# A mixture-of-experts stage with a written matmul order, smaller gather batches, more load buffers and another last norm

## The chip, the cores and the metric

The kernel runs on one core of one Trainium2 chip, as one program. The time is device microseconds of that core; lower is better. A time given is the median of repeated runs; the profile is one further execution with its own time. Engines are named as in the profile: PE is TensorE (PEld its weight loads), DVE VectorE, ACT ScalarE, POOL GpSimd, SP SyncE.

## The reference, cut to what matters

256 tokens of 1024 numbers pass through two dense blocks (feed-forward, state-space and attention mixers, feed-forward) and then a third block, whose end is what the change touches:

```python
h = h + ga1 * y                        # y: the mixer's output, merged @ w_out
u2 = rmsnorm(h, g_norm2) * (1 + sc2) + sh2
lg = u2 @ w_rg + b_rg                  # 4 groups
le = u2 @ w_re + b_re                  # 32 experts; top 2 inside the best group
comb = ...                             # (256, 32), two weights a token
for e in range(32):                    # D = 1024, d_expert = 512
    hid = silu(u2 @ w1[e]) * (u2 @ w3[e])
    y2 = y2 + comb[:, e:e+1] * (hid @ w2[e])
h = h + ga2 * y2
out = rmsnorm(h, g_final) * (1 + scf) + shf
```

All data are float32. Each of the 32 experts has three matrices of 2 MB, 192 MB in all.

## The kernel before

The dense blocks run from 0 to about 1517 us and are the same in both kernels but for the small reciprocal root (`rsqrt`, L71), which every norm calls. The products there are split into a high and a low part in a faster float32 format (three matmuls in place of one). What follows is the experts' stage.

**Loads.** `expert_loads` brings the 192 MB as 192 DMAs of 1 MB on SP's queue, in the order in which they are used: for each pair of experts w1 (4 loads), w3 (4), and w2 of the pair before (4). They go into a ring of buffers: 3 in `stream2`, 2 in `stream3`, 4 in `stream`, 3 in the stage's own pool (RAW2, RAW3, RAWB, RAW4), 12 in all. A load is issued when PE has read out what its buffer held before; `halves` asks for two new ones whenever two are used up.

**Before the first expert.** The last product of the mixer, with `w_out`, is made in two halves of 512 columns (L958 to L985). After each half DVE makes the new residual `x` and the gained rows `xg`, PE turns `xg` and multiplies it with the router's matrix (L980). Then `prep_end` makes `rstd`, DVE the router's logits `lg` (L989), `norm2` the normed rows: two DVE operations over 1024 columns (L1335), high parts on ACT (L1340), low parts on POOL (L1341). `route` picks two experts a token in some twenty small DVE operations (L1205 to L1241), and counts with two matmuls which of the 64 slots of an expert each token takes (`pos`). `gather` then makes a 0/1 matrix `sel` and with it, by matmul (L1431), the rows of 8 experts at a time, 64 slots each (CAP = 64, BATCH = 8), into a tile T.

**A pair of experts.** `project` multiplies w1 and then w3 with the gathered rows (L1469): one expert's 64 slots stand in the lower half of PE's columns and the other's in the upper half, so that matmuls of the two run side by side if they are issued one after the other. `hidden` turns the results (L1484) and makes silu times up; `down` multiplies with w2 of the pair before (L1504); ACT and DVE scale the result into a high and a low part (`yh` L1512, `yl` L1513); `spread` adds it to four PSUM tiles `acc` by eight matmuls with the turned 0/1 matrix (L1522). `slots` (L1446, L1448) makes that matrix and the slots' weights. PE's order in all this is chosen by a list scheduler at build time, which moves single matmuls into what it takes to be gaps; `beside` and `tick` offer it the gather and spread work.

**The end.** `finish` multiplies the four `acc` tiles by the gate `ga2` (L1365), jumps over the code for experts with more than 64 tokens (`overflow`, not entered with these inputs), adds to `x` (L1370, DVE), squares on ACT (L1371), multiplies by the gain on POOL (L1372), takes the root with `rsqrt` (12 small DVE operations), and makes the output in four pieces (L1377), stored by four DMAs (L1380). `finish_rows` loads and combines the rows for this on POOL while `route` runs.

Of the kernel before, what the change touches and what calls it, by code (L numbers as in the profile page):

```python
# [19 lines left out]
P = 128  # L20
D = 1024
# [5 lines left out]
NEXP = 32  # L27
CAP = 64
RAWB = 4
HLB = 3  # L30
RAW2 = 3
RAW3 = 2
RAW4 = 3
BATCH = 8
# [14 lines left out]
class Kern:  # L49
# [21 lines left out]
    def rsqrt(self, src, n, scale, pool=None):  # L71

        nc, pool = self.nc, pool or self.small
# [7 lines left out]
            y.bitcast(I32), t.bitcast(I32), -1.0, float(0x5F3759DF), op0=ALU.mult, op1=ALU.add  # L81
        )
        for _ in range(3):
            nc.vector.tensor_mul(t, y, y)  # L84
            nc.vector.scalar_tensor_tensor(t, t, -0.5, m, op0=ALU.mult, op1=ALU.mult)  # L85
            nc.vector.scalar_tensor_tensor(y, t, 1.5, y, op0=ALU.add, op1=ALU.mult)  # L86
# [742 lines left out]
    def mixer2(self):  # L829
        nc, a, tc = self.nc, self.a, self.tc  # L830
        w_in = a["w_in_2"][0]
        with ExitStack() as outer:
# [124 lines left out]
            self.ss = self.t(self.small, [P, 2, 2], "ss", bufs=2)  # L957
            pl = [self.t(self.ax, [P, 512], "ax") for _ in range(2)]  # L958
            xTs = self.t(keep, [P, 2, D], "o")
            for nb in range(2):  # L960
                sl = slice(nb * 512, (nb + 1) * 512)
                ps = self.gemm_x(a["w_out_2"][0], nb * 512, 512, self.xh, self.xl)
                xT = xTs[:, nb, :].rearrange("p (c t) -> p c t", c=4)
                done = None
                for t in range(2):
                    with tc.issue_after(done) if done else ExitStack():
                        m = self.t(self.tmp, [P, 512], "xg")
                        nc.vector.tensor_mul(m, ps[t], ga1[:, sl])
# [228 lines left out]
    def route(self, pool):  # L1197
# [36 lines left out]
        nc.vector.tensor_add(mb, o1, o2)  # L1234
# [3 lines left out]
        nc.tensor.matmul(pp[:, 32:64], self.ones, mb[:, 0, :], start=False, stop=True)  # L1238
        pos = self.t(pool, [P, 2, 32], "pos")
# [36 lines left out]
    def moe_begin(self):  # L1276
# [5 lines left out]
        w = self.t(self.s2, [P, 4, D], "T")  # L1282
        self.xg, self.sh2 = w[:, 0:2, :], w[:, 2, :]
        nc.gpsimd.dma_start(self.sh2, self.modd[0:1, 3 * D : 4 * D].to_broadcast([P, D]))
# [25 lines left out]
    def moe_final(self):  # L1310
        nc, a, tc = self.nc, self.a, self.tc
        with ExitStack() as ctx:
# [9 lines left out]
            route = self.route(lp)  # L1322
            self.norm2(lp, u2h, u2l)
            pos = next(route)
            rows = self.finish_rows(lp)
            comb, cnt = self.experts(lp, u2h, u2l, route, pos, acc)
            self.finish(lp, acc, rows, cnt, comb)

    def norm2(self, lp, u2h, u2l):

        nc = self.nc
        w = self.t(lp, [P, 4, D], "T")
        for t in range(2):
            u = w[:, t, :]
            nc.vector.scalar_tensor_tensor(  # L1335
                u.rearrange("p (k q) -> p q k", k=KD), self.xg[:, t, :].rearrange("p (q k) -> p q k", k=KD),
                self.rstd[:, t : t + 1], self.sh2.rearrange("p (q k) -> p q k", k=KD),
                op0=ALU.mult, op1=ALU.add,
            )
# [3 lines left out]
    def finish_rows(self, lp):  # L1343
# [14 lines left out]
    def finish(self, pool, acc, rows, cnt, comb):  # L1358
# [5 lines left out]
        for t, nb, sl in parts:  # L1364
            nc.vector.tensor_mul(y[:, t, sl], acc[t][nb], ga2[:, sl])  # L1365
# [437 lines left out]
```

## Time and profile before

| what | value |
|---|---|
| median of 3 runs | 2054.01 us (2053.54 to 2054.9) |
| the profiled execution's own time | 2053.34 us |
| its span, first to last instruction | 2051.6 us |
| PE busy | 1967.1 us (96%) |
| DVE, ACT, POOL busy | 1226.8, 882.6, 138.5 us |
| moved by DMA | 493.11 MB, mean 240 GB/s |

In the profile's page a line of 40 digits gives each engine's busy share in slices of 51 us; the experts' stage is the last ten slices. PE's digit is 9 in nearly all of the span, and since a matmul's record covers its whole way through the array, a 9 does not say that no time is lost between matmuls. In the last ten slices the DMA digit is 9 as well, with some 420 GB/s. Line numbers in rows of before are those of the kernel before.

### The profile page before, as it was taken

Reading aid. Unit: us, or ns where it says so; the run is one execution under the profiler, and the core shown is the slowest. Engines: PE = TensorE matmul, PEld = TensorE weight load, DVE = VectorE, ACT = ScalarE, POOL = GpSimd, SP = SyncE. Lnnn points to the kernel's source line nnn. Section 1 sums busy time; section 2 is a strip of 40 time slices with the busy share of each in tenths; the row PEclk is TensorE's granted clock in tenths of the full one; section 3 lists DMA queues with packets and bytes.
Section 4 is the critical chain, followed back from the end, with each engine's and each line's share of the span. In section 5 each row is a group of like instructions: output and inputs, shape, how many; then the busy total and the mean of one; then the engine's idle time right before and its main releaser. Section 6 shows DMA issues by size and latency. Waiting matters only on the chain. (4 is left out here: it accounts for less than half of the span.)

```text
span 2051.6 us, 25322 instructions
## 1 busy us (share of the span) xinstructions
PE 1967.1 (96%) x9734; PEld 1436.8 (70%) x9734; DVE 1226.8 (60%) x2099; ACT 882.6 (43%) x1318; POOL 138.5 (7%) x226
## 2 busy tenths in 40 slices
PE   8999999999999999999999999999969999999996
PEld 6888978788888888887788888978754333333332
DVE  5884897778867775698866555999772111110113
ACT  5444676654444444575745444576522101111101
POOL 1000222000000000014000000000120000000001
PEclk9999999999999999999999999999989999999998
DMA  8885543447776885642446556544766999999994
GB/s 281 280 283 185 166 144 103 154 155 266 263 258 207 266 271 182 196 150 97 133 144 204 179 164 204 177 148 140 244 261 269 422 414 378 421 369 420 421 421 172
DMA packets 193100, 493.11 MB, mean 240 GB/s; under 512 B 11832, under 2 KB 47600, under 8 KB 168400
## 3 DMA queue, kind: packets, MB, share of 16 engines
q1 hardware_dynamic: 185760, 479.32, 64.6%
q0 software_dynamic: 4992, 11.49, 1.7%
q8 instruction: 78, 1.28, 0.2%
q10 hardware_dynamic: 2224, 0.66, 0.2%
q14 instruction: 46, 0.38, 0.1%
HBM read 490.34 MB, written 1.08 MB: 240 GB/s over the span
## 5 line engine op out<-in xcount | busy, mean ns | idle before, releaser
L128 DVE TENSOR_TENSOR lo<-raw,hi 128x1024 fp32r<-128x1024 f32 (+1 forms) x462 | 563.6, 1221 | 280.4 <-ACT hi L127 279.4
L127 ACT ACTIVATE hi<-raw 128x1024 fp32r<-128x1024 f32 (+1 forms) x462 | 486.6, 1055 | 548.4 <-PE mm L174 477.9
L172 PE MATMUL mm<-hi,xh 128*128 128x512 f32 (+2 forms) x1200 | 463.9, 388 | 3.7 <-ACT hi L127 3.7
L173 PE MATMUL mm<-lo,xh 128*128 128x512 f32 (+2 forms) x1200 | 458.3, 382 | 0.4 <-DVE lo L128 0.4
L174 PE MATMUL mm<-hi,xl 128*128 128x512 f32 (+2 forms) x1200 | 457.8, 381 | 0.0
L172 PEld LDWEIGHTS mm<-hi,xh 128*128 128x128 f32 x1200 | 226.0, 189 | 49.2 <-ACT hi L127 4.6
L173 PEld LDWEIGHTS mm<-lo,xh 128*128 128x128 f32 x1200 | 226.2, 188 | 46.3 <-DVE lo L128 2.0
L174 PEld LDWEIGHTS mm<-hi,xl 128*128 128x128 f32 x1200 | 226.0, 188 | 46.0
L1469 PE MATMUL mm<-raw,T 128*64 128x512 f32 x1024 | 242.4, 596 | 0.0
L1469 PEld LDWEIGHTS mm<-raw,T 128*64 128x64 f32 x1024 | 72.9, 137 | 139.8 <-issue 137.0
L1504 PE MATMUL mm<-raw,H 128*64 128x512 f32 x512 | 148.6, 600 | 10.1 <-DVE gu L1474 10.1
L172 PE MATMUL mm<-hi,hh 128*128 128x512 f32 x352 | 139.1, 395 | 0.0
L174 PE MATMUL mm<-hi,hl 128*128 128x512 f32 x352 | 138.8, 394 | 0.0
L173 PE MATMUL mm<-lo,hh 128*128 128x512 f32 x352 | 138.5, 394 | 0.0
L1474 DVE COPY gu<-mm 128x512 f32<-128x512 f32 x16 | 11.1, 692 | 178.6 <-PE mm L1469 168.8
L1504 PEld LDWEIGHTS mm<-raw,H 128*64 128x64 f32 x512 | 45.9, 136 | 85.6 <-issue 63.3
L1512 ACT ACTIVATE yh<-mm,wsl 128x512 fp32r<-128x512 f32 x32 | 22.0, 687 | 181.7 <-PE mm L1504 181.7
L190 PE MATMUL mm<-xl,hi 128*128 128x256 f32 x320 | 90.0, 282 | 0.4 <-DVE xl L204 0.4
L189 PE MATMUL mm<-xh,hi 128*128 128x256 f32 x320 | 89.7, 282 | 0.0
L191 PE MATMUL mm<-xh,lo 128*128 128x256 f32 x320 | 89.7, 281 | 0.0
L759 DVE SCALAR_TENSOR_TENSOR macc<-raw,cact,macc 128x512 f32<-128x512 f32 x112 | 83.9, 750 | 2.2
L1513 DVE SCALAR_TENSOR_TENSOR yl<-mm,wsl,yh 128x512 fp32r<-128x512 f32 x32 | 24.0, 751 | 94.3 <-ACT yh L1512 93.0
(428 smaller groups left out, 2642.6 us busy)
## 6 DMA issues: line engine op xcount, KB each, us to landing
raw<-in_w_dram SPq DMA_DIRECT2D x192, 1024.0 KB, 10.2
raw<-in_w_in_dram SPq DMA_DIRECT2D x71, 1024.0 KB, 5.2
raw<-in_ffn_w_up_dram SPq DMA_DIRECT2D x44, 1024.0 KB, 7.0
raw<-in_ffn_w_gate_dram SPq DMA_DIRECT2D x43, 1024.0 KB, 5.2
raw<-in_ffn_w_down_dram SPq DMA_DIRECT2D x40, 1024.0 KB, 5.1
raw<-in_w_ada_dram SPq DMA_DIRECT2D x24, 1024.0 KB, 5.3
raw<-in_w_out_dram SPq DMA_DIRECT2D x20, 1024.0 KB, 5.1
raw<-in_w_ada_f_dram SPq DMA_DIRECT2D x8, 1024.0 KB, 5.3
```

What stands on the lines that cost most here:

```text
L127: nc.scalar.activation(h, r, AF.Copy)
L128: nc.vector.tensor_tensor(l, r, h.bitcast(F32), op=ALU.subtract)
L172: nc.tensor.matmul(ps[t][:, :w], xh[:, kc, sl], hi, start=kc == 0, stop=False)
L173: nc.tensor.matmul(ps[t][:, :w], xh[:, kc, sl], lo, start=False, stop=False)
L174: nc.tensor.matmul(ps[t][:, :w], xl[:, kc, sl], hi, start=False, stop=kc == kt - 1)
L189: nc.tensor.matmul(o, hi[:, sl], xh[:, kc, :], start=kc == 0, stop=False)
L190: nc.tensor.matmul(o, hi[:, sl], xl[:, kc, :], start=False, stop=False)
L191: nc.tensor.matmul(o, lo[:, sl], xh[:, kc, :], start=False, stop=kc == kt - 1)
L759: last = nc.vector.scalar_tensor_tensor(acc, raw[:, k, :], c, acc, op0=ALU.mult, op1=ALU.add)
L1469: nc.tensor.matmul(pg[s * CAP : (s + 1) * CAP, :], x[:, kc, s, :], w[:, k, :], start=kc == 0, stop=kc == KD - 1,)
L1504: nc.tensor.matmul(pd[nb][q, :], H[:, c, q], w[s][:, k, nb * 512 : (nb + 1) * 512], start=c == 0, stop=c == 3,)
L1513: nc.vector.scalar_tensor_tensor(yl, pd[nb], ws, yh.bitcast(F32), op0=ALU.mult, op1=ALU.subtract)
```

## The change

Front end: the second half of the `w_out` product is made in two quarters of 256 columns, with their own residual, turn and router matmuls. The shift `sh2` is no longer added to the normed rows, but per partition when the gathered rows leave PSUM (L1472, L1474 of the changed kernel), so that `norm2` is four ACT operations of 512 columns (high parts) and four DVE operations (low parts), placed after the choice of the experts; nothing of it is on POOL. `rsqrt` is 10 small operations where it was 12. Batches are of 4 experts (256 columns). The ring has 16 buffers (4, 2, 4, 6).

Experts: PE's instructions keep the order in which the code issues them, and `project`, `down` and `hidden` take hooks that say what stands between two blocks of eight matmuls. The gate `ga2` is multiplied in when `down`'s result leaves PSUM: DVE makes `y`, ACT its high part, DVE the low part.

End: the rows for the last norm are loaded by SP after the last expert's loads, in two buffers of the ring, and combined by one DVE operation; `acc` is added to `x` directly; the gain is multiplied by DVE; the overflow jump stands behind the stores, and redoes the norm if it is ever entered.

```diff
-RAW2 = 3
+RAW2 = 4
-RAW4 = 3
-BATCH = 8
+RAW4 = 6
+BATCH = 4
...
-            for nb in range(2):
-                sl = slice(nb * 512, (nb + 1) * 512)
-                ps = self.gemm_x(a["w_out_2"][0], nb * 512, 512, self.xh, self.xl)
+            for i, (c0, w) in enumerate(((0, 512), (512, 256), (768, 256))):
+                sl = slice(c0, c0 + w)
+                n = w // P
+                ps = self.gemm_x(a["w_out_2"][0], c0, w, self.xh, self.xl)
...
-    def norm2(self, lp, u2h, u2l):
...
-            nc.scalar.activation(u2h[:, t, :], u, AF.Copy)
-            nc.gpsimd.tensor_tensor(u2l[:, t, :], u, u2h[:, t, :].bitcast(F32), op=ALU.subtract)
...
+    def norm2(self, u2h, u2l):
...
+                nc.scalar.activation(h, u, AF.Copy, scale=r)
+                lows.append(low(h, u, l, r))
...
+        for dst, idx in ((Gf, 7), (shf, 6)):
+            nc.sync.dma_start(dst, self.modd[0:1, idx * D : (idx + 1) * D].to_broadcast([P, D]))
+        nc.sync.dma_start(g, a["g_final_2"].rearrange("(o n) -> o n", o=1).to_broadcast([P, D]))
+        nc.vector.scalar_tensor_tensor(Gf, Gf, 1.0, g, op0=ALU.add, op1=ALU.mult)
...
+        self.last_norm(acc, h, z, rows)
+        with self.tc.If(big > CAP):
+            self.overflow(pool, comb, h, z)
+            self.last_norm(None, h, z, rows)
...
-            nc.gpsimd.tensor_mul(y[:, t, sl], x, Gf[:, sl])
...
+            if acc:
+                nc.vector.tensor_add(y, acc[t][nb], self.x[:, t, sl])
...
-            yield i, (self.loaded.pop(0), self.loaded.pop(0))
-            self.refill(2)
-            self.tick()
+            self.refill(2)
+            for f in hooks[i] if hooks else ():
+                f()
...
-            nc.scalar.activation(yh, pd[nb], AF.Copy, scale=ws)
-            nc.vector.scalar_tensor_tensor(
-                yl, pd[nb], ws, yh.bitcast(F32), op0=ALU.mult, op1=ALU.subtract
-            )
+            nc.vector.scalar_tensor_tensor(
+                y, pd[nb], ws, self.ga2[:, nb * 512 : (nb + 1) * 512], op0=ALU.mult, op1=ALU.mult
+            )
+            nc.scalar.activation(yh, y, AF.Copy)
+            nc.vector.tensor_tensor(yl, y, yh.bitcast(F32), op=ALU.subtract)
...
+            gu.append(self.project(pool, x, on_scalar, [spread], [some(gat, 2 if ei else 3)]))
...
+            gu.append(
+                self.project(pool, x, nc.vector.tensor_copy, [some(turns, 1), some(slots, 1)], [])
+            )
             if last:
...
+                spread = self.down(
+                    pool, e - 2, last[0][0], *last[1], acc, [some(turns, 1), some(gat, 1)], [some(gat, 1)]
+                )
```

On PE, where a pair's spread (matmuls into `acc`) meets the next pair's w1 product (`raw`, `T` into `mm`; two raw numbers a block, one for each expert), the kernel before has this order:

```order
L1522 MATMUL acc_2625_13562<-yl_14985,selT_14730 128x512
L1522 MATMUL acc_2624_13561<-yh_14988,selT_14730 128x512
L1469 MATMUL mm_14998<-raw_14858,T_14253 64x512
L1522 MATMUL acc_2624_13561<-yl_14989,selT_14730 128x512
L1522 MATMUL acc_2626_13563<-yh_14988,selT_14730 128x512
L1522 MATMUL acc_2626_13563<-yl_14989,selT_14730 128x512
L1469 MATMUL mm_14998<-raw_14860,T_14253 64x512
L1469 MATMUL mm_14998<-raw_14858,T_14253 64x512
L1469 MATMUL mm_14998<-raw_14860,T_14253 64x512
L1469 MATMUL mm_14998<-raw_14858,T_14253 64x512
```

and the changed kernel this, for the same place in a later pair:

```order
L1506 MATMUL mm_15164<-raw_14971,T_14902 64x512
L1506 MATMUL mm_15164<-raw_14973,T_14902 64x512
L1558 MATMUL acc_2633_13589<-yh_15153,selT_14942 128x512
L1558 MATMUL acc_2633_13589<-yl_15154,selT_14942 128x512
L1558 MATMUL acc_2634_13590<-yh_15159,selT_14942 128x512
L1558 MATMUL acc_2634_13590<-yl_15160,selT_14942 128x512
L1558 MATMUL acc_2635_13591<-yh_15153,selT_14942 128x512
L1558 MATMUL acc_2635_13591<-yl_15154,selT_14942 128x512
L1558 MATMUL acc_2636_13592<-yh_15159,selT_14942 128x512
L1558 MATMUL acc_2636_13592<-yl_15160,selT_14942 128x512
L1506 MATMUL mm_15164<-raw_14995,T_14902 64x512
L1506 MATMUL mm_15164<-raw_14997,T_14902 64x512
```

The single w1 matmul inside the spread is gone; the spread stands whole between two blocks of eight, which begin and end with both experts.

On PE, where a pair's w3 product goes over into the w2 product (`H`), with the turn of the w3 result (`gu`) and the slots' matmuls, before:

```order
L1469 MATMUL mm_14906<-raw_14777,T_14253 64x512
L1469 MATMUL mm_14906<-raw_14779,T_14253 64x512
L1504 MATMUL mm_14952<-raw_14807,H_14795 64x512
L1504 MATMUL mm_14953<-raw_14807,H_14795 64x512
L1484 MATMUL tp_14992<-csq_66,gu_14943 128x128 x4
L1446 MATMUL tp_15015<-identr_320,sel_14238 128x128 x2
L1448 MATMUL tp_15015<-combs_13699,sel_14238 128x4 x2
L1504 MATMUL mm_14952<-raw_14809,H_14795 64x512
L1504 MATMUL mm_14952<-raw_14807,H_14795 64x512
L1504 MATMUL mm_14952<-raw_14809,H_14795 64x512
```

and after:

```order
L1506 MATMUL mm_15215<-raw_15046,T_14902 64x512
L1506 MATMUL mm_15215<-raw_15048,T_14902 64x512
L1539 MATMUL mm_15259<-raw_15073,H_15082 64x512
L1539 MATMUL mm_15259<-raw_15075,H_15082 64x512
L1539 MATMUL mm_15259<-raw_15073,H_15082 64x512
L1539 MATMUL mm_15259<-raw_15075,H_15082 64x512
L1539 MATMUL mm_15260<-raw_15073,H_15082 64x512
L1539 MATMUL mm_15260<-raw_15075,H_15082 64x512
L1539 MATMUL mm_15260<-raw_15073,H_15082 64x512
L1539 MATMUL mm_15260<-raw_15075,H_15082 64x512
L1520 MATMUL tp_15273<-csq_66,gu_15257 128x128 x4
L1466 MATMUL tp_15279<-sel_15197,u2h_13613 128x256 x2
```

Before, one expert's matmul for each of the two w2 tiles is issued ahead of the turn; after, a block of eight is, and the slots' matmuls have gone into the w3 product.

On DVE, from the router's logits `lg` to the choice of the group, before:

```order
L989 SCALAR_TENSOR_TENSOR lg_13536<-ax_13305,nw_y_13524,wr_13158 128x36
L989 SCALAR_TENSOR_TENSOR lg_13536<-ax_13306,nw_y_13524,wr_13158 128x36
L1335 SCALAR_TENSOR_TENSOR T_13580<-T_13150,nw_y_13524 128x128x8 x2
L1211 TENSOR_REDUCE rgm_13588<-lg_13536 128x2
L1212 TENSOR_TENSOR gu_13587<-lg_13536,rgm_13588 128x8
L1214 SCALAR_TENSOR_TENSOR gu_13587<-gu_13587,cmisc_318 128x8
```

and after:

```order
L998 SCALAR_TENSOR_TENSOR lg_13565<-ax_13270,nw_y_13555,wr_13123 128x36
L998 SCALAR_TENSOR_TENSOR lg_13565<-ax_13271,nw_y_13555,wr_13123 128x36
L1220 TENSOR_REDUCE rgm_13622<-lg_13565 128x2
L1221 TENSOR_TENSOR gu_13621<-lg_13565,rgm_13622 128x8
L1255 TENSOR_TENSOR rex_13744<-lg_13565,rgm_13622 128x8
L1223 SCALAR_TENSOR_TENSOR gu_13621<-gu_13621,cmisc_316 128x8
```

The two wide operations of `norm2` (128x128x8) no longer stand between the logits and the choice.

## Rows read from the trace of the kernel before

**Rows 1.** PE waits by releaser, 1545 to 2052: line waited for: us, times, longest

```profile
PE mm L1504 <- DVE gu L1474: 10.1, 13, 0.8
PE tp L1484 <- ACT gu L1534: 8.9, 13, 0.7
PEld mm L1469 <- DMA raw<-in_w_dram: 1.0, 3, 0.4
```

**Rows 2.** Waits of SP's queue, 1480 to 2052: us, times, longest

```profile
SPq L1392 <- PE mm L1469: 254.0, 113, 10.2
```

**Rows 3.** Busy time by stretch: us, PE PEld DVE ACT POOL, PEclk, DMA share, GB/s

```profile
1528.00:1555.00 27.00, 14.60 (x55) 9.75 (x55) 18.06 (x41) 5.53 (x10) 11.05 (x8) 0.67 0.07 20
1585.90:1990.00 404.10, 385.57 (x1630) 149.08 (x1628) 52.28 (x94) 44.84 (x76) 0.00 (x0) 1.00 0.99 408
...
1845.00:2015.00 170.00, 161.25 (x688) 60.37 (x687) 18.68 (x36) 17.71 (x30) 0.00 (x0) 1.00 1.01 421
```

**Rows 4.** Timeline of PE, one pair without gather: start, us, instruction, [idle before]

```profile
1966.14 1.07 PE L1469 MATMUL mm<-raw,T 128*64 128x512 f32 x2
...
1975.80 0.74 PE L1484 MATMUL tp<-csq,gu 128*128 128x128 f32 x4 [0.68 <-ACT gu L1534]
...
1984.34 1.07 PE L1504 MATMUL mm<-raw,H 128*64 128x512 f32 x2 [0.78 <-DVE gu L1474]
...
1994.74 1.07 PE L1469 MATMUL mm<-raw,T 128*64 128x512 f32 x2
```

**Rows 5.** Timeline of PE between the last dense product and the experts

```profile
1516.57 0.39 PE L174 MATMUL mm<-hi,xl 128*128 128x512 f32 x1
...
1539.75 0.69 PE L1237 MATMUL mm<-gu,csq 128*128 128x64 f32 x2 [15.69 <-DVE gu L1234]
...
1541.95 1.62 PE L1431 MATMUL acc<-sel,u2h 128*128 128x512 f32 x3 [0.65 <-DVE sel L1417]
...
1551.36 1.08 PE L1469 MATMUL mm<-raw,T 128*64 128x512 f32 x4
```

**Rows 6.** Timeline of DVE and POOL in the same stretch

```profile
1524.27 3.77 DVE L1335 SCALAR_TENSOR_TENSOR T<-T,nw_y 128x1024 f32<-128x1024 f32 x2
...
1527.40 5.02 POOL L1341 TENSOR_TENSOR u2l<-T,u2h 128x1024 fp32r<-128x1024 f32 x2 [6.09 <-ACT u2h L1340]
...
1527.88 0.16 DVE L1211 TENSOR_REDUCE rgm<-lg 128x2 f32<-128x8 f32 x1
1528.10 2.05 DVE L1212 TENSOR_TENSOR gu<-lg,rgm 128x8 f32<-128x8 f32 x1
...
1530.18 2.27 DVE L1214 SCALAR_TENSOR_TENSOR gu<-gu,cmisc 128x8 f32<-128x8 f32 x1
...
1534.24 0.51 DVE L1214 SCALAR_TENSOR_TENSOR gu<-gu,cmisc 128x64 f32<-128x64 f32 x1
...
1536.36 1.57 DVE L1214 SCALAR_TENSOR_TENSOR gu<-gu,cmisc 128x64 f32<-128x64 f32 x1
...
1538.22 1.21 DVE L1217 TENSOR_TENSOR gu<-cmisc,r2f 128x64 f32<-128x64 f32 x1
```

**Rows 7.** Timeline of SP's queue at the start of the experts

```profile
1516.99 1.28 SPq L1392 DMA_DIRECT2D raw<-in_w_dram  x3
...
1555.04 4.92 SPq L1392 DMA_DIRECT2D raw<-in_w_dram  x4
```

**Rows 8.** The load's line, 1530 to 1600: time from issue to landing

```profile
DMA to landing us min/median/max: 5.2/9.3/12.1
```

**Rows 9.** Timeline of PE, DVE and POOL at the end

```profile
2024.91 7.09 PE L1504 MATMUL mm<-raw,H 128*64 128x512 f32 x30
...
2036.13 4.64 DVE L1370 TENSOR_TENSOR x<-x,T 128x512 f32<-128x512 f32 x4
2036.99 6.12 POOL L1372 TENSOR_TENSOR T<-x,fin 128x512 f32<-128x512 f32 x4 [497.64 <-DVE x L1370]
...
2045.51 2.74 DVE L1377 SCALAR_TENSOR_TENSOR T<-T,nw_y,fin 128x512 f32<-128x512 f32 x4 [0.21 <-DVE nw_y L86]
```

More of the change, by code (lines that the diff above doesn't have):

```diff
@@ L27 @@
 NEXP = 32
+RC = 0.375**0.2
 CAP = 64
@@ L1321, in moe_final @@
             u2l = self.t(lp, [P, 2, D], "u2l", F32R)
-            route = self.route(lp)
-            self.norm2(lp, u2h, u2l)
+            self.ga2 = self.load_row(lp, self.modd[0:1, 5 * D : 6 * D], D, "ga2")
+            lows = self.norm2(u2h, u2l)
+            route = self.route(lp, lows)
             pos = next(route)
-            rows = self.finish_rows(lp)
-            comb, cnt = self.experts(lp, u2h, u2l, route, pos, acc)
+            with tc.manual_schedule(engines={mybir.EngineType.PE}):
+                comb, cnt, rows = self.experts(lp, u2h, u2l, lows, route, pos, acc)
@@ L1534, in on_scalar, with some, none @@
             nc.scalar.activation(d, s, AF.Copy)
-        batch, last = [], None
-        nxt = self.beside(self.gather(pool, 0, u2h, u2l, pos, batch, acc[0] + acc[1]))
-        sel0 = next(nxt[0])
+        def some(gen, n):
+            return lambda: [next(gen, None) for _ in range(n)]
+        def none():
+            pass
+        batch, last, spread = [], None, none
+        gat = self.gather(pool, 0, u2h, u2l, pos, batch, acc[0] + acc[1], lows)
         for e in range(0, NEXP, 2):
@@ L1541, in experts @@
             if ei == 0:
-                self.drain(nxt)
+                for _ in gat:
+                    pass
                 sel, T = batch
-                if e == 0:
-                    with self.tc.issue_after(sel0):
-                        comb, combs, cnt = next(route)
-                batch = []
+                batch, gat = [], iter(())
                 if b + 1 < NEXP // BATCH:
-                    nxt = self.beside(paced(self.gather(pool, b + 1, u2h, u2l, pos, batch), 2, 1))
-            so, h = [], []
+                    gat = self.gather(pool, b + 1, u2h, u2l, pos, batch)
@@ L1551, in experts @@
+            so, h, gu = [], [], []
             x = T[:, :, ei : ei + 2, :]
-            slots = self.beside(self.slots(pool, sel, ei, e, combs, so))
-            gu = [self.project(pool, x, on_scalar)]
-            gu.append(self.project(pool, x, nc.vector.tensor_copy))
-            self.drain(slots)
-            hid = self.hidden(pool, gu, h)
-            next(hid)
-            if last:
-                self.down(pool, e - 2, last[0][0], *last[1], acc)
-            for _ in hid:
-                pass
@@ new lines, in experts @@
+            turns = self.hidden(pool, gu, h)
+            filled = self.filled
+            gu.append(self.project(pool, x, on_scalar, [spread], [some(gat, 2 if ei else 3)]))
+            if e == 0:
+                with self.tc.issue_after(filled):
+                    comb, combs, cnt = next(route)
+            slots = self.slots(pool, sel, ei, e, combs, so)
+            gu.append(
+                self.project(pool, x, nc.vector.tensor_copy, [some(turns, 1), some(slots, 1)], [])
+            )
```

317 lines of the change are left out of this document (164 added, 153 removed).

## The prediction

> **What bounds the kernel now.** I read the table of waits first, then the busy times by stretch, then PE's timeline over one pair of experts, and last the two places where PE has nothing to do: ahead of the experts and at the end.
>
> In the experts' stage the waits [rows 1] show that PE waits for a load 3 times and 1.0 us in all, while SP's queue stands 254.0 us, in 113 waits, until PE has read a w1 or w3 buffer out [rows 2]. So PE is late and the loads wait for it. The reader is to see, however, how thin the lead is: the DMA share is 0.99 over 404 us at 408 GB/s, and over the last 170 us it is 1.01 at 421 GB/s [rows 3]. The stage runs from 1551.36 [rows 5] to the end of the last w2 matmul at 2024.91 + 7.09 = 2032.0 [rows 9]: 480 us for 16 pairs, 30.0 us a pair. A pair loads 12 x 1.049 MB = 12.58 MB, and at 421 GB/s that takes 29.9 us. PE and the loads are equal within half a per cent. Whatever makes PE faster here is given back as soon as the loads' lead is used up.
>
> Ahead of the experts PE stands 15.69 us, until the choice of experts is made, and then makes all rows of 8 experts by matmul, from 1541.95 to 1551.36, before the first w1 product [rows 5]. In that time the loads rest too: SP issues three at 1517 and the next at 1555.04 [rows 7], and the DMA share from 1528 to 1555 is 0.07 [rows 3]. If the loads are the bound afterwards, this hole is what counts.
>
> **Front end.** Before, the last `w_out` matmul begins at 1516.57 [rows 5], the logits are done at about 1524.4, and then two operations of `norm2`, 3.77 us together, stand on DVE ahead of `route`, which starts at 1527.88 [rows 6]. `route` ends with the count at 1539.75: 11.9 us. While POOL makes low parts (5.02 us and more), small DVE operations are slow: 2.05 and 2.27 us for 128x8, where 0.16 is the price of the one before them; 1.57 and 1.21 us for 128x64, where 0.51 stands between them [rows 6]. The excess in these four is 1.9 + 2.1 + 1.1 + 0.7 = 5.8 us. After, `norm2` has no POOL operation and follows the choice, so `route` takes 11.9 - 5.8 = 6.1 us, and the 3.8 us ahead of it go. The quarters of `w_out` shorten the way from the last matmul to the logits: one turn and router product of 256 columns in place of 512, which I put at -2.2 us from the 7.8 us that it takes now, and +0.4 us for the smaller matmuls. Choice and count are then done at 1524.4 - 1.8 + 6.1 = 1528.7, and with 2.1 us for `pos` and `sel` as before the gather begins at 1530.8.
>
> The gather of 8 experts took 9.4 us. The clock granted from 1528 to 1555 is 0.67 on average [rows 3]; with levels of 1 and one half that is some 18 us at the lower one, so until about 1546, and the first 3.8 us of the gather cost 1.9 more than at full clock. At full clock it is 7.5 us, for 4 experts 3.8; with the clock's 1.9 (PE still stands about 12 us ahead of it) and 0.4 for the last copy out of PSUM it is 6.1. The first w1 product starts at **1536.9**, 14.5 us earlier. Bounds: -10 if the half chunk gains nothing and the high parts on ACT are late, -17 if the clock stays up.
>
> **The stage, on PE.** A pair without gather takes 1994.74 - 1966.14 = 28.6 us, with waits of 0.68 for the turn's input and 0.78 for the w3 result in it [rows 4]; there are 13 of each in all [rows 1]. The written order puts a block of w2 in front of the turn and the slots' work into w3: the w3 result's copy, about 1.4 us, is then covered by the block's first eight matmuls, 16 records and 3.5 us (half of 7.09 [rows 9]). So 1.5 us go. The scheduler also leaves four single-expert matmuls a pair, whose half of the columns runs alone (the piece of the order in the section on the change shows one in the spread): four slots of two records at 0.22 us, 1.7 us. The gather is not in this pair; at 7.5 us for four pairs it adds 1.9. With about 0.4 for other switches between kinds of matmul I estimate 28.6 - 1.5 - 1.7 + 1.9 + 0.4 = **27.7 us a pair**. The gate's operation adds one DVE operation of 0.7 us to each of two results a pair; `y`, `yh`, `yl` in a row are 2.1 us, twice, and the spread follows a w1 block later (3.5 us): hidden. If it isn't, it shows as PE waiting for `yl`.
>
> **The stage, on the loads.** 27.7 is less than 29.9, so the loads become the bound. 16 buffers (they are full at the start, since PE reads none for over 20 us) leave 176 loads. The first can be issued when a block of w1 is read, 3.7 us after the start, at 1540.6, and lands 5.2 us later [rows 8], at 1545.8. The other 175 follow at 1.0486 MB / 420 GB/s = 2.50 us: 437 us, last landing **1982.8**. PE can't lag: what it needs for the last loads is the spread of the pair before and a block of w2 of 3.5 us, so the last matmul begins some 4.2 us after the landing and ends at 1987.6. Bounds of the rate: 408 GB/s, the mean of the stage before with SP's stalls in it, gives 2.57 us a load and +13 us; 421 gives -1.
>
> The Trainium skill ("DMA: Bandwidth & Descriptors", section "Where 436 GB/s comes from") says that for transfers from HBM the limit of one core's share, about 358 GB/s, binds, and not the 435 of the ports. By that a load would take 2.93 us and 175 of them 513 us. The trace doesn't agree: 421 GB/s over 170 us, all of it read from HBM [rows 3]; the measurement decides.
>
> **The end.** Before, 2051.6 - 2032.0 = 19.6 us. After: `y` 0.7, `yh` 0.7, `yl` 0.7 (a quarter of 2.74 for each 512 columns [rows 9]), the combined gain row over 1024 columns 1.4, three adds to `x` 2.05 (the first stands in front of `yl`, where DVE waits for ACT), two products by the gain 1.4, the sum 0.2, two more products 1.4 among the root's 10 operations of 0.2 each (2.0), the four final ones 2.74 [rows 9], and from there to the end 3.35 as before. Sum 16.65, with 0.15 for hand-overs 16.8: **-2.8 us**. What goes is the add of 4.64 us for four, slowed beside POOL's 6.12 us [rows 9]. The three loads for the rows stand behind the last expert load and land some 4 us after it, while their reader comes 7 us after it: not late. The jump behind the stores costs 0 to 1.5.
>
> **Sum.** 1987.6 + 16.8 = 2004.4 for the span; the profiled execution has 2053.34 for a span of 2051.6, so +1.74: 2006.1; the median is 0.67 above that execution: **2007**.
>
> **Rivals.**
> *PE stays the bound.* If blocks, switches and the smaller gather batches cost as much as the scheduler's gaps, PE keeps its 30.0 us: 1536.9 + 480 + 0.6 + 16.8 + 2.4 = **2037**. For it: more instructions of 256 columns, and an order that can't slip round a late operand. Against: 3.2 us a pair are visible losses that the order names.
> *PE stands at every block (slower).* In the written order, five places a pair depend on a result of DVE or ACT, and nothing else can be issued there. If each costs the 0.78 of the wait in [rows 4], a pair takes 27.7 + 3.9 = 31.6 us: 1536.9 + 505.6 + 0.6 + 16.8 + 2.4 = **2062**. It decides from 31.1 us a pair, 0.68 at each of the five. Against: the operands are made a block, 3.5 us, before their use, and the longest chain is 2.1.
> *The clock falls.* When PE waits for loads, the granted clock may fall to 1.2 GHz. Before, only the hole of 15.69 us lowered it [rows 3, 5]; waits of 0.78 left it at 1.00 over 404 us. After, the waits would be (29.9 - 27.7) / 6, about 0.4 at each of six half matrices. A fall as long as that of the front costs 1.9 us, and at that rate PE has no waits left and makes them up only over a pair; three or so unhidden ones give **2012**.
> The Trainium skill ("TensorE: Matmul & The Clock Gate", section "HAM oscillation — how this bites in real kernels") tells of a kernel that waits for DMA in every tile and starts each at the lower clock; by it all the stage might run so. At half clock PE would need 55 us a pair, which no load waits for, so it can't last.
>
> **How the numbers follow.** The forecast, loads bound from about 1541 on, 2000 to 2015: 0.68. PE at 30.0 or between (2015 to 2040): 0.16. The clock: 0.05, in or near the first band. Better than 2000, by a shorter front and 421 GB/s: 0.05. No change, since front and order both give nothing: 0.02. PE at each block: 0.04. The range from 1999 to 2030 leaves out the far end of the second case and the slower one. A difference under 0.2% can't be told from none in such a measurement. Faster 0.94, same 0.02, slower 0.04.
>
> **What would show it.** Right: the first w1 product near 1537; a DMA share of 1 and some 420 GB/s from 1541 to 1983; waits of PE for `raw` that appear and grow, and few of SP for PE; no small DVE operation over 0.6 us in `route`; an end of about 17 us. Wrong: SP still waiting 250 us for PE (the first rival), PE waiting for `gu`, `yl` or `T` at each block (the second), a granted clock below 1 in the stage (the third), or a mean rate near 408 GB/s although the queue is never empty.

## The result and the profile after

| | before | after |
|---|---|---|
| median | 2054.45 us (2053.54 to 2056.23) | 2003.63 us (2003.4 to 2004.11) |
| ratio, 95% interval | | 0.9752 [0.9735, 0.9769] |
| profiled execution, span | 2053.34, 2051.6 | 2003.45, 2001.6 |

The change is worth 50.8 us; 47 were forecast, and the 2007 us of the forecast are 3.4 us above the time. I read the traces at four marks, which split the span:

| mark, us | before | forecast | after |
|---|---|---|---|
| first w1 product starts | 1551.36 | 1536.9 | 1533.29 |
| last load lands | 2019.95 | 1982.8 | 1980.06 |
| last w2 product ends | 2032.0 | 1987.6 | 1984.39 |
| end of the span | 2051.6 | 2004.4 | 2001.6 |

So 18.1 us came from the stretch ahead of the experts, 29.5 from their stage (480.6 to 451.1 us), 2.4 from the end. In the forecast these were 14.5, 29.9 and 2.8.

The waits come first again, as in [rows 1, 2]: line waited for, us in total, times, longest. PE's weight loads (PEld) run ahead of the products, so their waits are longer than what PE loses by them.

```profile
PEld mm L1539 <- DMA raw<-in_w_dram: 10.5, 8, 2.0
PEld mm L1506 <- DMA raw<-in_w_dram: 6.3, 10, 2.0
PE mm L1539 <- DMA raw<-in_w_dram: 4.1, 6, 1.1
...
PEld mm L1539 <- DVE gu L1511: 2.0, 7, 0.3
...
PE mm L1506 <- DMA raw<-in_w_dram: 1.1, 1, 1.1
```

And SP's queue:

```profile
SPq L1421 <- DMA raw<-in_w_dram: 248.5, 121, 3.6
SPq L1421 <- PE mm L1506: 98.2, 28, 16.9
```

The roles have changed places. The w2 product no longer waits on PE for the w3 result (10.1 us in [rows 1]; 2.0 us of PEld are left); PE now waits for loads, and SP, which stood 254.0 us for w1 and w3 products [rows 2], stands 98.2 us for them and 248.5 us for loads that it has issued and that are not in yet. A load takes 19.8 us from issue to landing in the median, so at 2.5 us a load some eight are under way. Busy time by stretch (columns as in [rows 3]):

```profile
1521.00:1541.00 20.00, 15.38 (x74) 10.07 (x74) 12.31 (x37) 7.66 (x13) 0.00 (x0) 0.72 0.71 283
1541.00:1980.00 439.00, 432.27 (x2021) 185.74 (x2020) 85.77 (x167) 56.23 (x108) 0.00 (x0) 1.00 1.01 421
```

From 1541 to 1980 the DMA share is 1.01 at 421 GB/s without a break; before, the stage's mean was 408 [rows 3]. POOL is at zero in both stretches. The granted clock stays 1.00 although PE waits for loads, up to 1.1 us at a time.

A piece of PE's timeline in the stage, to be held against [rows 4] (start, us, instruction, idle before it in brackets):

```profile
1752.94 3.65 PE L1506 MATMUL mm<-raw,T 128*64 128x512 f32 x16
1756.53 0.75 PE L1520 MATMUL tp<-csq,gu 128*128 128x128 f32 x4
...
1757.55 3.65 PE L1506 MATMUL mm<-raw,T 128*64 128x512 f32 x16
1761.03 3.60 PE L1539 MATMUL mm<-raw,H 128*64 128x512 f32 x16
1764.57 0.75 PE L1520 MATMUL tp<-csq,gu 128*128 128x128 f32 x4
...
1765.72 3.65 PE L1539 MATMUL mm<-raw,H 128*64 128x512 f32 x16
...
1769.96 3.65 PE L1506 MATMUL mm<-raw,T 128*64 128x512 f32 x16
```

Every block is whole, 16 records in 3.65 us, and no row of this piece has a bracket: the turn follows its block with no wait, where [rows 4] shows 0.68 and 0.78. Ahead of the experts (PE, then DVE; to be held against [rows 5, 6]):

```profile
1514.94 0.28 PE L180 MATMUL mm<-hi,xl 128*128 128x256 f32 x1
...
1524.76 0.69 PE L1246 MATMUL mm<-gu,csq 128*128 128x64 f32 x2 [5.05 <-DVE gu L1243]
...
1526.69 2.17 PE L1466 MATMUL acc<-sel,u2h 128*128 128x256 f32 x8 [0.87 <-DVE sel L1447]
...
1533.29 7.09 PE L1506 MATMUL mm<-raw,T 128*64 128x512 f32 x32
```

```profile
1519.94 0.42 DVE L998 SCALAR_TENSOR_TENSOR lg<-ax,nw_y,wr 128x36 f32<-128x36 f32 x2
1520.39 0.16 DVE L1220 TENSOR_REDUCE rgm<-lg 128x2 f32<-128x8 f32 x1
1520.59 0.17 DVE L1221 TENSOR_TENSOR gu<-lg,rgm 128x8 f32<-128x8 f32 x1
...
1523.70 0.23 DVE L1223 SCALAR_TENSOR_TENSOR gu<-gu,cmisc 128x64 f32<-128x64 f32 x1
```

The choice of experts takes 1524.76 - 1520.39 = 4.4 us instead of 11.9, and no operation in it is over 0.23 us. The end, on PE and DVE:

```profile
1980.73 3.65 PE L1539 MATMUL mm<-raw,H 128*64 128x512 f32 x16
```

```profile
1986.94 1.22 DVE L1374 SCALAR_TENSOR_TENSOR raw<-raw,raw 128x1024 f32<-128x1024 f32 x1
1988.08 1.88 DVE L1395 TENSOR_TENSOR u2h<-acc,x 128x512 f32<-128x512 f32 x3
1989.88 1.28 DVE L1404 TENSOR_TENSOR u2h<-u2h,raw 128x512 f32<-128x512 f32 x2
...
1994.19 2.74 DVE L1406 SCALAR_TENSOR_TENSOR u2l<-u2h,nw_y,raw 128x512 f32<-128x512 f32 x4
```

Where [rows 9] has 4.64 us for the four adds, three take 1.88; the first ran ahead of `yl`. The last four operations are the same 2.74 us.

### The profile page after: what moved, and what is told of

Read it like the earlier page. It is cut to its first block, busy times and chain, and to the rows that moved or that the text cites. A ratio compares the mean times of both kernels' runs of the same rounds, so it can differ in the third digit from the quotient of the medians.

```text
span 2001.6 us, 25699 instructions
## 1 busy us (share of the span) xinstructions
PE 1946.9 (97%) x9910; PEld 1451.0 (72%) x9910; DVE 1238.0 (62%) x2122; ACT 887.8 (44%) x1342; POOL 119.8 (6%) x212
## 4 chain that ended last, share of the span: by engine, by line
PE 83%; DMA 6%; DVE 6%; ACT 2%; issue 1%; POOL 0%; SPq 0%; DVEq 0%; ACTq 0%
PE mm L178 18%; PE mm L180 18%; PE mm L179 18%; PE mm L1506 9%; DMA raw<-in_w_dram 6%; PE mm L1539 4%; PE tp L206 2%; PE mm L196 2%; PE mm L197 2%; PE mm L195 2%; DVE lo L134 2%; PE tp L1466 1%; PE acc L1558 1%; PE tp L1520 1%; PE ax L720 1%
## 5 line engine op out<-in xcount | busy, mean ns | idle before, releaser
L178 PE MATMUL mm<-hi,xh 128*128 128x512 f32 (+1 forms) x1216 | 467.5, 386 | 3.4 <-ACT hi L133 3.3
L179 PE MATMUL mm<-lo,xh 128*128 128x512 f32 (+1 forms) x1216 | 461.7, 380 | 0.2 <-DVE lo L134 0.2
L180 PE MATMUL mm<-hi,xl 128*128 128x512 f32 (+1 forms) x1216 | 460.5, 379 | 0.0
L1539 PE MATMUL mm<-raw,H 128*64 128x512 f32 x512 | 124.3, 597 | 4.1 <-DMA raw<-in_w_dram 4.1
L195 PE MATMUL mm<-xh,hi 128*128 128x256 f32 x320 | 89.8, 283 | 0.0
L197 PE MATMUL mm<-xh,lo 128*128 128x256 f32 x320 | 89.8, 281 | 0.0
L1472 DVE TENSOR_SCALAR T<-tp,cact 128x256 f32<-128x256 f32 x28 | 13.4, 479 | 116.1 <-PE tp L1466 116.1
L180 PEld LDWEIGHTS mm<-hi,hl 128*128 128x128 f32 x352 | 66.2, 188 | 15.2
L179 PEld LDWEIGHTS mm<-lo,hh 128*128 128x128 f32 x352 | 66.2, 188 | 14.9
## 6 DMA issues: line engine op xcount, KB each, us to landing
raw<-in_w_dram SPq DMA_DIRECT2D x192, 1024.0 KB, 19.8
```

Source lines behind the costliest of these rows:

```text
L178: nc.tensor.matmul(ps[t][:, :w], xh[:, kc, sl], hi, start=kc == 0, stop=False)
L179: nc.tensor.matmul(ps[t][:, :w], xh[:, kc, sl], lo, start=False, stop=False)
L180: nc.tensor.matmul(ps[t][:, :w], xl[:, kc, sl], hi, start=False, stop=kc == kt - 1)
L195: nc.tensor.matmul(o, hi[:, sl], xh[:, kc, :], start=kc == 0, stop=False)
L197: nc.tensor.matmul(o, lo[:, sl], xh[:, kc, :], start=False, stop=kc == kt - 1)
L1539: nc.tensor.matmul(pd[nb][q, :], H[:, c, q], w[s][:, k, nb * 512 : (nb + 1) * 512], start=c == 0, stop=c == 3,)
```

## The experiments

My theory was that PE's scheduled order bounds the kernel before and the loads bound the changed one; the rival, that PE bounds both. Marks of all runs, from their traces, "end" being the time from the last w2 product to the end of the span:

| kernel | median us | first w1 | stage | end |
|---|---|---|---|---|
| before | 2054.45 | 1551.4 | 480.6 | 19.6 |
| after | 2003.63 | 1533.3 | 451.1 | 17.2 |
| 1 after, fewer loads | 1985.05 | 1535.2 | 432.4 | 16.7 |
| 2 after, scheduled | 2067.38 | 1534.2 | 513.6 | 17.7 |
| 3 scheduled, fewer loads | 2012.12 | 1533.9 | 459.1 | 17.0 |
| 4 before, fewer loads | 2037.49 | 1553.3 | 464.0 | 19.9 |
| 5 after, 12 buffers | 2015.04 | 1533.8 | 461.2 | 17.1 |
| 6 low parts first | 2008.99 | 1539.2 | 450.9 | 17.2 |
| 7 low parts on POOL | 2011.45 | 1542.0 | 451.4 | 17.2 |
| 8 gain on POOL | 2005.85 | 1535.5 | 451.2 | 18.3 |
| 9 written order alone | 2027.9 | 1545.5 | 461.1 | 18.3 |
| 10 all but written order | 2042.49 | 1539.5 | 484.7 | 17.7 |
| 11 w2 on a second queue | 2022.4 | 1533.1 | 469.9 | 16.5 |
| 12 earlier first block | 2006.21 | 1531.5 | 452.2 | 19.2 |

The end of the dense blocks, whose code these kernels share, lies between 1514 and 1519 us in the single profiled executions, so a first w1 product is known to some 2 us only; the stage and the end are not touched by that.

**1. Fewer loads.**

```diff
-                for s in range(2):
+                for s in range(1 if nmk == "w2_2" else 2):
...
-            yield i, (self.loaded.pop(0), self.loaded.pop(0))
-            self.refill(2)
+            r = self.loaded.pop(0)
+            yield i, (r, r if one else self.loaded.pop(0))
+            self.refill(1 if one else 2)
...
```

> The changed kernel, but w2 is loaded for one expert of each pair and used for both: 160 loads of 1 MB in place of 192, every matmul kept (the result is that of other weights). Theory (the loads bound the changed kernel): the first w1 product stays at 1533, 143 loads after the first are in by about 1900, PE stands for no load, and what remains is PE's own pace: 451.1 us of stage less the 22.0 us for which PE stands for loads, 429 us, so about 1982 in all. Rival (PE is still the bound, and its waits for loads are only where it would have stood anyway): 2003, no change.

1985.05 us, ratio to before 0.9661 [0.9644, 0.9677], below the interval of the change itself. Nothing on PE was taken away, its matmuls come in the same order in both traces, and no wait for a load is left in its list. So the loads bind the changed kernel, for 451.1 - 432.4 = 18.7 us of it. PE's own pace is 432.4 / 16 = 27.0 us a pair. The 22.0 us that I had taken off were PE's and PEld's waits added up, and these overlap. PE's own list has 5.2 us of waits for loads in the changed kernel; the rest of the 18.7 lies inside blocks that take longer.

**2. Scheduled order.**

```diff
-            with tc.manual_schedule(engines={mybir.EngineType.PE}):
+            if True:
```

> The changed kernel with the order of PE's instructions left to the scheduler again; buffers, batches of 4, front and end as changed. Theory (the scheduler's gaps hold PE at 30 us a pair, more than the loads need): stage 480 us in place of 451, about 2032. Rival (the written order is worth nothing, because a scheduled PE at 28 to 29.5 us a pair would be under the loads' 29.9 as well): 2003 to 2006, and the waits for loads shrink.

2067.38, ratio 1.0063 [1.0046, 1.0079]: slower than before. The direction is the theory's, the size isn't: 32.1 us a pair, not 30. The old waits are back (PE's list, and SP's queue, which stands for PE again while PE waits for no load):

```profile
PE mm L1539 <- DVE gu L1511: 9.3, 12, 0.8
PE tp L1520 <- ACT gu L1572: 8.9, 12, 0.7
PE tp L1466 <- DVE H L1525: 3.4, 11, 0.3
...
SPq L1421 <- PE mm L1506: 251.8, 105, 17.1
```

and the timeline shows where they stand, with blocks in pieces between:

```profile
1761.10 0.59 PE L1539 MATMUL mm<-raw,H 128*64 128x512 f32 x1
1761.53 0.59 PE L1506 MATMUL mm<-raw,T 128*64 128x512 f32 x1
...
1762.90 1.07 PE L1539 MATMUL mm<-raw,H 128*64 128x512 f32 x2 [0.78 <-DVE gu L1511]
...
1765.44 0.39 PE L1466 MATMUL tp<-sel,u2h 128*128 128x256 f32 x1 [0.31 <-DVE H L1525]
```

The gather's matmuls of 256 columns, which the written order keeps in fours behind whole blocks, are strewn singly here. A matmul of one expert alone keeps PE for 0.43 us (1761.10 to 1761.53), where a whole block has 16 in 3.65. So the written order is worth 64 us against this scheduled one, and with this one the rest of the change, with its batches of 4 and 16 buffers, is a loss.

**3 and 4. Fewer loads with a scheduled PE.** The edit is that of the first experiment, in the scheduled kernel and in the kernel before.

> Scheduled order and 160 loads together. Theory: PE sets the time with either number of loads, so within 4 us of the scheduled kernel with all loads, about 2030; against the written order with 160 loads (about 1982) the whole price of the scheduled order, some 48 us, is seen. Rival (loads bound the scheduled kernel too): 20 us or more below it.

> The kernel before with 160 loads, by the same edit. Theory (PE bounds the kernel before, its waits for loads are 1.0 us in all): 2053, no change that can be told. Rival (a DMA share of 0.99 means that the loads bound it too): 20 us or more faster.

Both missed: 2012.12, 55 us under the scheduled kernel with all loads, and 2037.49, ratio 0.9916 [0.99, 0.9933]. The edit changed two things, because with fewer loads the scheduler made another order of PE's instructions: the matmuls of the two traces come in another order in both cases, unlike in (1). PE's list of the fourth kernel shows it too: the w2 product's wait for the w3 result, 10.1 us before [rows 1], has no line there; of the others this one stays.

```profile
PE tp L1485 <- ACT gu L1535: 6.1, 9, 0.7
```

The traces speak against the loads as the cause: the waits of PE and PEld for loads in the stage are 1.0 us before and 1.8 in (4), and there are none in (2) and (3). Where the time went is seen when PE's records are added up from the first w1 to the last w2 product, each from its start to the next start, less the idle time between (us):

| kernel | idle | the experts' 1536 matmuls | all others |
|---|---|---|---|
| before | 20.0 | 373.5 | 87.1 |
| 4 before, fewer loads | 6.3 | 368.6 | 89.0 |
| 2 after, scheduled | 23.6 | 389.5 | 100.4 |
| 3 scheduled, fewer loads | 5.2 | 361.7 | 92.1 |
| 1 after, fewer loads | 1.5 | 341.0 | 89.8 |

PE's instructions in (1), (2) and (3) are the same in number and shape. So one scheduled order costs 17 or 55 us more than another, in waits and in matmuls that stand alone, and the written one has the least of both. No run keeps an old order with fewer loads; that the loads had no part in the 17 and 55 us is read from the waits alone.

**5. Twelve buffers.**

```diff
-RAW2 = 4
+RAW2 = 3
 RAW3 = 2
-RAW4 = 6
+RAW4 = 3
```

> The changed kernel with 12 buffers as before (3, 2, 4, 3) in place of 16. Theory (from the first freed buffer to the last load the time is loads left times 2.49 us): four more loads are left at 1537, +10.0 us, 2013.6; the DMA share ahead of 1537 falls and PE's waits for loads grow from 22 to some 32 us. Rival (more buffers only smooth the flow, which is even already): 2003 to 2005.

2015.04: +11.4 us, the stage 10.1 longer, with PE's matmuls in the same order. Four loads at 2.5 us each: as the theory has it.

**6 and 7. The low parts ahead of the choice, on DVE, and on POOL.**

```diff
-            lows = self.norm2(u2h, u2l)
+            for low in self.norm2(u2h, u2l):
+                low()
+            lows = []
...
```

```diff
-                nc.scalar.activation(h, u, AF.Copy, scale=r)
-                lows.append(low(h, u, l, r))
+                nc.vector.tensor_scalar(u, u, r, None, op0=ALU.mult)
+                nc.scalar.activation(h, u, AF.Copy)
+                nc.gpsimd.tensor_tensor(l, u, h.bitcast(F32), op=ALU.subtract)
...
```

> The changed kernel with the four DVE operations of norm2 ahead of the choice of experts, still on DVE. Theory (what delays the first w1 product delays the first freed buffer, and with it every load left): they take 1.14 us each, 4 x 1.1 = 4.5 us; but the gather no longer stands behind two of them; first product 3 to 4.5 us later and the time longer by the same, 2007 to 2008. Rival (16 buffers hide a late start, or the loads catch up): under 1 us.

> The changed kernel with norm2 as before on three engines: normed rows on DVE ahead of the choice, high parts on ACT, low parts on POOL beside it. Theory: the choice takes 4.4 us now and 11.9 us beside POOL's work in the kernel before; four DVE operations of 512 columns add about 2.5 to 4 us; so the first product comes some 8 to 11 us later and the time is 2012 to 2015. Rival (the slow operations of before came from DVE's own queue, not from POOL): as with the low parts first on DVE, 2006 to 2008.

2008.99 (+5.4) and 2011.45 (+7.8). The first product is 5.9 and 8.7 us later (1.1 and 2.4 of it since the dense blocks ended later in these executions) and the stage unchanged within 0.4: a microsecond ahead of the experts costs one at the end, in spite of the 16 buffers. The second kernel's choice of experts beside POOL, in DVE's and POOL's timelines:

```profile
1525.19 0.15 DVE L1220 TENSOR_REDUCE rgm<-lg 128x2 f32<-128x8 f32 x1
1525.38 1.30 DVE L1221 TENSOR_TENSOR gu<-lg,rgm 128x8 f32<-128x8 f32 x1
...
1526.71 1.45 DVE L1223 SCALAR_TENSOR_TENSOR gu<-gu,cmisc 128x8 f32<-128x8 f32 x1
1528.19 0.16 DVE L1225 TENSOR_REDUCE rgf<-gu 128x2 f32<-128x8 f32 x1
...
1531.45 0.23 DVE L1221 TENSOR_TENSOR gu<-gu,r1m 128x64 f32<-128x64 f32 x1
```

```profile
1524.77 6.30 POOL L1362 TENSOR_TENSOR u2l<-T,u2h 128x512 fp32r<-128x512 f32 x4 [50.01 <-ACT u2h L1361]
```

Until 1531.07, when POOL is done, operations that take 0.17 us in the changed kernel take 1.30 and 1.45; those of 128x64 take 0.23 afterwards. That is the mechanism read from [rows 6], now made at will. ACT isn't the cause: in the changed kernel it made the high parts beside the choice as well (1519.86 to 1524.39), and no operation of the choice was over 0.23. The reduces, with one input, keep 0.15 and 0.16. The Trainium skill ("GPSIMD Engine Reference", section "1. Specifications") says that GpSimd shares its memory interfaces with VectorE, where that has two inputs or a fast mode; by this row the trace agrees.

**8. The gain on POOL.**

```diff
-            nc.vector.tensor_mul(h[:, t, sl], h[:, t, sl], Gf[:, sl])
+            nc.gpsimd.tensor_mul(h[:, t, sl], h[:, t, sl], Gf[:, sl])
```

> The changed kernel with the four products by the gain row in the last norm on POOL again, beside the root on DVE. Theory: POOL takes about 1.5 us for each (6.12 us for four in the kernel before), and the small operations of the root beside it are slower; the end grows by 2 to 4 us, 2006 to 2007. Rival (the products are off the path, since the root takes 2 us anyway, and POOL starts them as each sum is there): 2003 to 2004.

2005.85 (2003.46 to 2007.04), and the end 18.3 us in place of 17.2: +1.1, less than I expected; the time alone doesn't tell it, the trace does. Two operations of the root meet POOL; the products themselves are off the path.

```profile
1993.34 1.14 DVE L79 TENSOR_SCALAR nw_m<-ss 128x2 f32<-128x2 f32 x1
1994.51 1.19 DVE L82 TENSOR_SCALAR nw_t<-nw_m 128x2 int32<-128x2 int32 x1
1995.73 0.17 DVE L83 TENSOR_SCALAR nw_y<-nw_t 128x2 int32<-128x2 int32 x1
```

**9 and 10. The written order alone, and all the rest without it.** The ninth has BATCH = 8, RAW2 = RAW4 = 3 and the edits of 7 and 8; the tenth has BATCH = 8, RAW2 = RAW4 = 3 and the edit of 2. Common to both:

```diff
-RAW2 = 4
+RAW2 = 3
 RAW3 = 2
-RAW4 = 6
-BATCH = 4
+RAW4 = 3
+BATCH = 8
```

> The changed kernel with nearly all but the written order put back: 12 buffers, batches of 8, norm2 on three engines ahead of the choice, the gain on POOL. (The quarters of w_out, the gate in the experts' outputs and the place of the rows and of the jump stay as changed.) Theory (the scheduled order, not the number of buffers, holds the kernel before at 30 us a pair; with the written order the loads bind): first product near 1544, first load after it lands 8.7 us later, 179 more at 2.49 us to about 1998, the last matmul 4.4 us behind, an end of 18.3: 2023. Rival (written order gives little with 12 buffers and the late start): 2037 to 2045.

> Its counterpart: the new front and end, but PE scheduled, batches of 8 and 12 buffers as before. Theory (with batches of 8 the scheduler finds what it found in the kernel before, 30.0 us a pair): first product near 1537.5, 480.6 us, an end of 17.2, 2037. Rival (the scheduler's order is worse with the gate's new operation in the chain, whatever the batch: the 32.1 us a pair of the scheduled kernel with batches of 4): 2070.

2027.9, ratio 0.9871 [0.9856, 0.9886], and 2042.49, ratio 0.9939 [0.9924, 0.9954]. The written order with the old rest is worth 26.6 us, the new front and end with the old order 12. Their sum is 38.5, and the whole change gave 50.8. The four further buffers and the batches of 4 are in neither kernel, and the buffers alone are worth 11.4 us (5), nearly all that is missing. What the buffers give under a scheduled PE wasn't tried. From the ninth to the changed kernel it adds up: 24.3 us, of which 11.4 are the buffers (5), 7.8 the low parts (7), 1.1 the gain (8) and 4.8 the shorter first gather (10.6 us from its first matmul to the first w1 product, against 5.8 in 7), 25.1 in all. The ninth is loads bound already:

```profile
1560.00:1960.00 400.00, 387.48 (x1702) 158.32 (x1699) 71.73 (x126) 44.56 (x80) 0.00 (x0) 1.00 1.01 421
```

It came 5 us later than I had worked out: 1.5 at the start, 2.8 more until the last load is in (2002.4 us), and the rest between the profiled execution's span and the median. In the tenth the stage is 484.7 us, near the 480.6 of before, so the gate's operation is not what makes the scheduled order bad in 2; the change from batches of 8 and 12 buffers to 4 and 16 is, the only difference between the two. Which of the two wasn't tried.

**11. A second queue.**

```diff
-                    self.nc.sync.dma_start(
+                    (self.nc.gpsimd if nmk == "w2_2" else self.nc.sync).dma_start(
```

> The changed kernel with the 64 loads of w2 issued by POOL on its own queue, the others by SP as now. Theory (the 16 DMA engines are full, share 1.01 at 421 GB/s, so a second queue adds nothing): 2002 to 2006. Rival (one queue limits the rate): the last load lands earlier, down to PE's own pace of 27.0 us a pair, 1985.

2022.4, slower than the change by 18.8. The rate is the same, and the last load is in 4.1 us later (1984.16):

```profile
1541.00:1980.00 439.00, 423.81 (x1970) 179.66 (x1968) 81.32 (x159) 54.97 (x105) 32.27 (x62) 1.00 1.01 421
```

One queue therefore doesn't limit it, as the theory says. What it costs stands in PE's list, the second line in a single wait near the end:

```profile
PE mm L1506 <- DMA raw<-in_w_dram: 13.0, 10, 3.9
PE mm L1539 <- DVE gu L1511: 6.9, 1, 6.9
```

Loads of two queues no longer land in the order of use: PE waits 13.0 us for w1 and w3, where the changed kernel has 1.1 for them and 4.1 for w2. The 6.9 us have another cause. On DVE, whose order the scheduler still chooses, the operation that combines the rows of the last norm (L1374) stands here ahead of the copy of the last w3 result (L1511), and waits for the rows' load:

```profile
1984.15 1.23 DVE L1374 SCALAR_TENSOR_TENSOR raw<-raw,raw 128x1024 f32<-128x1024 f32 x1 [29.55 <-DMA raw<-in_g_final_dram]
```

In the changed kernel it comes behind the last `yl`, at 1986.94. So the order of arrival costs 13.0 - 5.2 = 7.8 of the 18.8 us in waits, and this order on DVE 6.9. The other 4 us are in the matmuls themselves; the clock has a part in it, which fell to its lower level here, at the end of the wait of 3.9 us and in the wait of 6.9:

```profile
1972.20:1975.60 3.40, 2.96 (x8) 1.00 (x10) 0.00 (x0) 0.00 (x0) 0.00 (x0) 0.50 1.04 425
1982.40:1989.30 6.90, 2.91 (x8) 0.76 (x8) 2.14 (x4) 0.00 (x0) 0.00 (x0) 0.51 0.05 20
```

**12. An earlier first block.** The gather of the first batch stops ahead of its last eight matmuls, which follow the first half of w1; the spread moves behind the last product.

```diff
+                if banks and k0 and n == 0:
+                    yield
...
-                for _ in gat:
-                    pass
+                first, n_first = gat, 3 if e == 0 else 99
+                for _ in zip(range(n_first), gat):
+                    pass
...
-            gu.append(self.project(pool, x, on_scalar, [spread], [some(gat, 2 if ei else 3)]))
+            gu.append(self.project(pool, x, on_scalar, [some(first, 1), spread], [some(gat, 2 if ei else 3)]))
...
-        spread_end = self.down(pool, NEXP - 2, last[0][0], *last[1], acc, [spread], [])
+        spread_end = self.down(pool, NEXP - 2, last[0][0], *last[1], acc, [], [spread])
```

> The changed kernel with two places of the written order moved: the first half of the first pair's w1 product ahead of the last eight gather matmuls, and the spread of the last but one pair behind the last product in place of between its halves. Theory (the first freed buffer sets all loads after it): first load issued 1 to 1.5 us earlier, though the second pair of loads comes 0.5 to 1 us later; the last product starts 0.6 us nearer to its load, and the added spread hides beside the chain of y, yh and yl: 2001.5 to 2002.7. Rival (the second pair's delay eats it, or the first block waits for the gathered rows): 2003 to 2005.

2006.21 (2004.73 to 2007.57), no gain. The first load goes out at 1535.22 instead of 1536.96, but the third at 1539.94 instead of 1540.40, and the last lands at 1980.05, as without the edit. The dense blocks ended 0.9 us earlier in this execution, so the edit itself brought the first load 0.9 us forward and put the third 0.4 back. The end is 2.0 us longer. `yh` and `yl` have two buffers each, which come free only when the spread of the pair before has read them, and that spread now begins behind the last product; so the last pair's `yl` begins at 1985.84, where the changed kernel has it at 1984.23:

```profile
1983.67 0.50 PE L1560 MATMUL acc<-yh,selT 128*128 128x512 f32 x1
```

```profile
1985.84 0.69 DVE L1554 TENSOR_TENSOR yl<-gu,yh 128x512 fp32r<-128x512 f32 x1 [1.32 <-ACT yh L1553]
```

In the changed kernel that spread filled the time in which the last load was on its way. So no kernel here beats the changed one with all loads.

## Why the prediction was right, step by step

**Loads become the bound: right.** Shown by (1), (5) and the stretch of 439 us. The sum's terms: first load 3.67 us after the first product (3.7 worked out), landing 5.0 us later (5.2), 175 loads in 438.1 us (437), the last product 4.3 us behind the last landing (4.8). The slower bound, 408 GB/s, didn't come: it was SP standing for PE.

**PE's pace of 27.7 us a pair: right within 0.7.** (1) measures 27.0. The two things that were to go, the waits and the single-expert matmuls, are gone from the timeline. By the table of (3) and (4), from before to (1), the waits gave (20.0 - 1.5) / 16 = 1.2 us a pair (1.5 worked out) and the experts' matmuls (373.5 - 341.0) / 16 = 2.0 (1.7). What a scheduled order costs varies: the same instructions need 32.1 us a pair in (2) and 28.7 in (3), where 30.0 stood in the rows that I read.

**Front: the mechanism right, the size 3.6 us short.** First product 1533.29, not 1536.9. Of this 2.2 is at the logits: 1520.4 and not 1522.6, where the dense blocks ended 2.0 us earlier than I had set them, which is inside what they vary. 1.7 is `route`: I took away the excess of the four slowest operations, but operations of 0.51 us beside POOL were slow too (0.23 now), so 4.4 and not 6.1 us. Two of the four, the 1.57 and 1.21 of [rows 6], stood not beside the low parts but beside POOL's work on the rows for the last norm, which the change took away as well. The gather took 6.6, not 6.1: the clock was at its lower level until 1532.2, for 5.5 us of it, which costs 2.8 and not 1.9, while the last copy added nothing. At full clock that leaves the 3.8 worked out. Its granted clock:

```profile
1526.69:1533.29 6.60, 6.60 (x33) 6.21 (x33) 5.24 (x9) 1.53 (x4) 0.00 (x0) 0.58 0.82 346
```

**End: the sum right, by two errors that nearly cancel.** 17.2 us against 16.8 from the last product. Up to the four final operations it took 9.8 us, where 10.7 were worked out. From the last of these to the end of the span it took 4.65, where I had put 3.35 as before: the last store takes 2.9 us from issue to landing instead of 2.1, and from its landing to the end 1.7 us pass instead of 1.1. The prediction has 0 to 1.5 us for the jump behind the stores, but not in the sum.

**The rivals.** PE as the bound falls with (1). PE standing at each block falls with the waits: for `gu` 2.0 us of PEld, for `yh` and `yl` 3.0. The falling clock: 1.00 over the stage, with waits of up to 1.1 us; the front has 0.72. It fell within the stage in (11) alone, where PE waited 3.9 and 6.9 us at a time. The limit of 358 GB/s that the Trainium skill names ("DMA: Bandwidth & Descriptors", section "Where 436 GB/s comes from") doesn't show here either: 421 GB/s for 439 us.

**What stays open.** Why the scheduled order needs 32.1 us a pair with batches of 4 and 16 buffers and 30.3 with 8 and 12. Added up as in the table, PE is idle as long in both, 23.6 and 23.2 us; (2) has 16 us more in the experts' matmuls and 13 more in the gather's. Whether the batches or the buffers lead the scheduler to it, no run shows.

## What to carry to other kernels

Where two resources are within a per cent of each other, ask what each would take alone: here PE had 27.0 us a pair in it and the loads 29.9, and the 30.0 that stood in the profile hid both. Once the loads bind, every microsecond before the first freed buffer and every buffer short costs its full price (1 us, and 2.5), while PE's order has slack; so the order of repairs matters, and a part can be worth nothing or less alone (the scheduled kernel with the rest of the change was 13 us slower than before). An edit of loads under a scheduler changes the order as well, so it doesn't isolate the loads: fix the order first, and look at every engine whose order is still free (in 11 it was DVE's).

## What was not expected of the hardware

While POOL works on two tensors, a small DVE operation with two inputs ended within 0.1 us of the end of one of POOL's. In (7) these take 1.88, 1.50, 1.50 and 1.50 us, so four DVE operations of 0.17 to 0.23 took 1.24 to 1.50; a fifth, which began at 1526.60, where one of POOL's ended, took 0.15. In (8) two operations with one input (`TENSOR_SCALAR`, 1.14 and 1.19 us) are slowed alike, while the reduces of (7) are not, and three adds that read `acc` in PSUM took 1.88 us beside POOL in (8), as in the changed kernel. What POOL does matters: before, beside its `TENSOR_SCALAR`, such operations of DVE took 0.22 to 0.56 us, and only beside its `TENSOR_TENSOR` 1.21 to 2.27 (POOL, then DVE, with the 1.57 of [rows 6] next):

```profile
1535.08 1.53 POOL L1354 TENSOR_SCALAR fin<-fin 128x512 f32<-128x512 f32 x1
1536.60 1.25 POOL L1355 TENSOR_TENSOR fin<-fin,gu 128x512 f32<-128x512 f32 x1
```

```profile
1536.10 0.22 DVE L1212 TENSOR_TENSOR gu<-gu,r2m 128x64 f32<-128x64 f32 x1
```

And a rate of 421 GB/s for 439 us was kept with one queue or two, but with two the order of arrival was lost, at a price of some 8 us in waits for loads.
